# A float32 decoder trunk on one core: other start addresses for the matmuls' moving tiles, and gate and up products issued as three of 256 columns

## The chip, the cores and the metric

The kernel is one program on one core of a Trainium2 chip. The metric is the device time of one execution in microseconds (us), lower is better. In what follows PE is TensorE with its weight loads as PEld, DVE is VectorE, ACT is ScalarE, POOL is GpSimd, and SP is the engine that issues the weight transfers.

## The reference

Four layers work on 256 tokens of width 1024, all in float32. Each layer is a half-weighted SwiGLU feed-forward block, a token mixer, and a second feed-forward block:

```python
for i in range(DEPTH):                      # DEPTH = 4
    kind, j = i % N_MIXERS, i // N_MIXERS   # mixers: 0 gated DeltaNet, 1 stick-breaking, 2 sparse (DSA)
    x = x + 0.5 * swiglu(rmsnorm(x, ffn1_norm[i]), ffn1_w_gu[i], ffn1_w_down[i])
    h = rmsnorm(x, mix_norm[i])
    m = (gated_deltanet, stick_breaking_attention, dsa_sparse_attention)[kind](h, ...)
    x = x + m
    x = x + 0.5 * swiglu(rmsnorm(x, ffn2_norm[i]), ffn2_w_gu[i], ffn2_w_down[i])
return rmsnorm(x, final_norm)

def swiglu(h, w_gu, w_down):                # D_MODEL = 1024, D_FF = 2816
    gate, up = jnp.split(h @ w_gu, 2, axis=-1)
    return (jax.nn.silu(gate) * up) @ w_down
```

The mixers run in the order DeltaNet, stick-breaking, sparse, DeltaNet. Each has an input projection, attention-like work on 8 heads of 128, and an output projection 1024 to 1024.

## The kernel before

Everything is kept transposed, features on the 128 partitions and the 256 tokens along the free dimension. A float32 product is made exact enough from two float32r parts: an operand is split into `hi` and `lo`, and three products, `hi*hi + lo*hi + hi*lo`, are summed in PSUM. So each 128 by 128 weight tile with 256 tokens takes 768 columns of moving data.

**Weights.** Each chunk of 128 x 2048 weights (1 MB) arrives by one transfer on SP's queue into a tile `r` (3 buffers). It is split in four pieces of 512 columns: ACT writes `h` (L170), DVE writes `l` (L171), from pools `hi` and `lo` of 10 buffers each. A piece serves four k tiles of a gate or up product, or four row tiles of a down product.

**Activations.** `norm_in` writes x times the gain as one tile `x2` of 8 k tiles, each with 256 columns of hi beside 256 of lo; the trace calls it `x`. The hidden activations of a feed-forward block are `ah` and `al`, the heads' outputs of a mixer `oh` and `ol`, the latents of the sparse mixer `lath` and `latl`.

**Products.** The weight piece is the stationary operand and the activation the moving one. There are three forms:

- `tile_wide` makes the gate and up products: for each of 8 k tiles, the `h` weights against 512 columns (hi and lo of x side by side), then the `l` weights against 256 columns, into a PSUM bank of tag G.
- `rows` makes the down products and the output projections: for each tile three products of 256 columns (`mm3`), `ah` with `h`, `ah` with `l`, `al` with `h`. The same function serves the feed-forward blocks, which accumulate in four banks of tag A, and the mixers' `out_proj`, which accumulates `oh` and `ol` in four banks of tag G.
- `tiles2` makes the mixers' input projections: three products of 256 columns with `x2`, into banks of tag G.

Only the values of the stick-breaking mixer have it the other way round: there x is stationary and the weights move, 512 columns at a time.

**Order.** A feed-forward block is 11 steps of 256 hidden columns. A step (L346 to L361) is two chunks of gate and up products, 32 k tiles, and one chunk of down products of the step before, 48 products. Mixer work is written as generators that advance between groups of the big products (`pump`), by a count of PE's columns. Within an engine the instructions stand in the order that a scheduler gives them when the program is built; the engine then runs them in that order. The chain of small operations in a mixer is: rstd of the tokens, gates, keys with a triangular inverse, queries, the delta rule per head pair, then `out_proj`.

**Places in SBUF.** Tiles lie in pools, one behind the other. In the built program before, modulo 512 bytes, `h`, `l`, `x2`, `oh`, `ol`, `lath` and `latl` all start at 352, `ah` and `al` at 32, and the small weight tiles `bah`, `wih` and `wil` at 0. All slices that the big products take of them begin a multiple of 512 bytes further on, except in the sparse mixer's key projection.

Of the kernel before, what the change touches and what calls it, by code (L numbers as in the profile page):

```python
# [20 lines left out]
P = 128  # L21
T = 256          # tokens
D = 1024
KT = D // P      # k tiles of the model width
F = 2816
NS = F // 256    # steps of a feed-forward block, 256 hidden columns each
# [3 lines left out]
RS = 1024.0      # scale of the residuals kept in float16  # L30

# Everything is kept transposed: [feature on partitions, token].  A float32 matmul operand x is split
# exactly into hi = x rounded to float32r and lo = x - hi; hi*hi + lo*hi + hi*lo in PSUM carries float32.


class Bank:
    """One PSUM bank that several accumulation groups share."""
# [16 lines left out]
    def tr(self, out, x):  # L54
        """Transposes a [128, 128] float32 tile; the only kind of write to its part of the bank."""
        self.nc.tensor.transpose(out, x, self.k.ident)  # L56
        self.k.now += 0.11
# [8 lines left out]
class Trunk:  # L66

    def __init__(self, tc, ctx, a):
# [6 lines left out]
        self.lop = pool(name="lo", bufs=10)  # L75
        self.big = pool(name="big", bufs=8)
        self.wk = pool(name="wk", bufs=2)
# [20 lines left out]
    def table(self, name):  # L98
        """A mixer's constants, side by side."""
        t = self.wk.tile([P, 1024], F32, name="tab", tag="tab", bufs=1)  # L100
        src = self.a[name]
        self.nc.sync.dma_start(t[:, :src.shape[1]], src)
        return t
# [13 lines left out]
    def bank(self, tag="A"):  # L117
        """A: small products and a feed-forward's sums; G: the big projections."""
        return Bank(self, self.ps.tile([P, 512], F32, name="bank" + tag, tag=tag))

    # ---- interleaving: side work (generators) advances between groups of the big products.  A generator
    # yields how long (us on TensorE's clock, as counted here) its next stage's operands are expected to take,
    # or a condition that its next stage waits for.
# [6 lines left out]
    def pump(self, n=None):  # L130
        """Run up to n ready stages; only the first few (width) generators are under way."""
# [13 lines left out]
    def wait(self, done):  # L145
        """Run side work until done()."""
# [13 lines left out]
    def chunk(self, src, w=2048, pw=512, pool=(), parts=1):  # L160
        """A [128, w] chunk of weights as (hi, lo) pieces of pw columns; the pieces in pool are split by GpSimd."""
# [12 lines left out]
    def first_chunk(self, src, n):  # L174
        """The kernel's start: the first chunk and x arrive in parts and are split as they come."""
# [27 lines left out]
    def rsqrt(self, a, n):  # L203
        """Newton's iteration for a ** -0.5 on a small tile."""
# [20 lines left out]
    def norm_in(self, n):  # L225
        """x times the gain, split; the tokens' factors come later (rstd)."""
# [5 lines left out]
    def spread(self, cols):  # L232
        """[token, 1] columns (SBUF) -> a bank with each as a row on all partitions."""
# [5 lines left out]
    def rstd(self, st):  # L239
        """1 / rms(x) per token, into st: compact [token, 2] and as rows [128, T]."""  # L240
# [28 lines left out]
    # GDN's chunks of the input projection, (kind, head pair): keys 0, values 1, queries 2, gate 3  # L269
    gdn_order = ((0, 0), (0, 1), (0, 2), (3, 0), (0, 3), (3, 1), (2, 0), (1, 0), (1, 1), (1, 2), (1, 3),  # L270
                 (2, 1), (3, 2), (2, 2), (2, 3), (3, 3))
    korder = (0, 2, 4, 6, 1, 3, 5, 7)    # the order in which a block's last products finish x

    def tiles2(self, pieces, xg, order=None):
        """Two M tiles (8 k tiles each) of one chunk into one bank."""
# [8 lines left out]
    def tile_wide(self, pieces, m, order=None):  # L284
        """One M tile into a bank: the columns of hi * hi and those of hi * lo + lo * hi side by side."""
        b = self.bank("G")
        for q, j in enumerate(order or self.korder):
            wh, wl = self.sub(pieces, m * D + j * P, P)
            b.mm(b.t, wh, self.x2[:, j], False)
            b.mm(b.t[:, T:], wl, self.x2[:, j, :T], q == KT - 1)  # L290
# [4 lines left out]
    def rows(self, acc, pieces, a2, last, done=None):  # L295
        """acc[d, t] += w[f, d] a[f, t] for the chunk's two k tiles."""
# [910 lines left out]
```

## Time and profile before

| | |
|---|---|
| time, median of 3 runs | 2089.17 us (2088.93 to 2093.96) |
| the profiled execution: span from its first to its last instruction | 2092.3 us |
| PE busy | 97% of the span, 14762 matmuls |
| PEld, DVE, ACT busy | 90%, 79%, 63% |
| transfers | 353.62 MB, 169 GB/s on average |
| mean granted TensorE clock | 0.993 of full speed |

The span is the profiled execution's own time as far as it is listed. A busy share says how long an engine had something under way; matmuls overlap each other in it, so that what one matmul costs is read from the distance between the starts of two that follow each other, and not from its duration.

### The profile page before, as it was taken

What the parts mean: (1) busy time and instruction counts of PE and PEld (TensorE: products, weight loads), DVE (VectorE), ACT (ScalarE), POOL (GpSimd) and SP (SyncE); (2) the same over time, 40 slices, a digit from 0 to 9 for tenths busy, and PEclk for the clock granted to TensorE, in tenths of its full rate; (3) what the DMA queues carried; (4) which work ended last, traced back from release to release, by engine and by line L of the source; (5) the groups of instructions that cost most, each with busy time, mean ns of one, the idle gap of its engine ahead of it and who ended that gap; (6) DMA issues with size and microseconds to landing.
All of it is one profiled execution on the core that took longest, in us unless ns stands there. A gap on an engine that the chain in (4) does not pass through costs nothing.

```text
span 2092.3 us, 38898 instructions
## 1 busy us (share of the span) xinstructions
PE 2037.1 (97%) x14762; PEld 1886.2 (90%) x14762; DVE 1646.0 (79%) x3456; ACT 1308.2 (63%) x2804; POOL 161.9 (8%) x145
## 2 busy tenths in 40 slices
PE   8999899999999999999999998999999998999998
PEld 7999899999999989999989997899989998999997
DVE  7778898877887776777787789877787788988776
ACT  6566776665665566655665664765665667766654
POOL 1001311100100010100010013100010013111000
PEclk9999999999999999999999999999999999999999
DMA  7555333555455554555555542455555553235552
GB/s 256 195 188 182 102 105 123 173 190 187 171 206 188 195 179 140 176 184 197 185 184 199 182 153 76 162 187 196 184 182 199 184 179 106 100 119 182 182 199 84
DMA packets 52603, 353.62 MB, mean 169 GB/s; under 512 B 6976, under 2 KB 7872, under 8 KB 10688
## 3 DMA queue, kind: packets, MB, share of 16 engines
q1 hardware_dynamic: 52128, 350.49, 48.4%
q8 instruction: 116, 1.90, 0.4%
q14 instruction: 71, 0.58, 0.1%
q10 hardware_dynamic: 288, 0.66, 0.1%
HBM read 350.07 MB, written 1.05 MB: 168 GB/s over the span
## 4 chain that ended last, share of the span: by engine, by line
PE 82%; DVE 12%; ACT 4%; issue 1%; POOL 0%; DMA 0%; SPq 0%; ACTq 0%; DVEq 0%; POOLq 0%
PE bankG L43 55%; PE bankA L43 25%; DVE l L171 5%; ACT x L222 1%; DVE kT L466 1%; PE bankA L56 1%; ACT h L170 1%; DVE x L223 1%; DVE rs_t L211 1%; DVE x L302 0%; DVE rs_y L212 0%; DVE rs_t L210 0%; ACT sq L244 0%; DVE vT L466 0%; DVE pc L455 0%
## 5 line engine op out<-in xcount | busy, mean ns | idle before, releaser
L43 PE MATMUL bankG<-x,h 128*128 128x512 f32 (+1 forms) x4192 | 1269.0, 361 | 12.0 <-DVE x L223 12.0
L171 DVE TENSOR_TENSOR l<-r,h 128x512 fp32r<-128x512 f32 x1328 | 936.7, 713 | 374.1 <-ACT h L170 370.9
L170 ACT ACTIVATE h<-r 128x512 fp32r<-128x512 f32 x1328 | 823.0, 627 | 595.5 <-PE bankG L43 337.4
L43 PE MATMUL bankG<-x,l 128*128 128x256 f32 x3504 | 989.2, 282 | 0.0
L43 PEld LDWEIGHTS bankG<-x,h 128*128 128x128 f32 x4192 | 751.3, 189 | 130.1 <-DVE x L223 14.9
L43 PEld LDWEIGHTS bankG<-x,l 128*128 128x128 f32 x3504 | 666.5, 190 | 0.1
L43 PE MATMUL bankA<-ah,l 128*128 128x256 f32 x1408 | 389.2, 276 | 0.0
L43 PE MATMUL bankA<-ah,h 128*128 128x256 f32 x1408 | 389.2, 276 | 0.0
L43 PE MATMUL bankA<-al,h 128*128 128x256 f32 x1408 | 389.1, 276 | 0.0
L43 PEld LDWEIGHTS bankA<-ah,h 128*128 128x128 f32 x1408 | 264.4, 188 | 3.3
L43 PEld LDWEIGHTS bankA<-al,h 128*128 128x128 f32 x1408 | 264.5, 188 | 0.0
L43 PEld LDWEIGHTS bankA<-ah,l 128*128 128x128 f32 x1408 | 264.4, 188 | 0.0
L330 DVE TENSOR_TENSOR e<-e,bankG 128x256 f32<-128x256 f32 x352 | 145.9, 414 | 4.6 <-ACT e L329 4.6
L329 ACT ACTIVATE e<-bankG 128x256 f32<-128x256 f32 x352 | 129.3, 367 | 11.5 <-PE bankG L43 11.5
L245 POOL TENSOR_TENSOR sq<-sq 128x512 f32<-128x512 f32 x12 | 15.5, 1294 | 1473.8 <-ACT sq L244 1473.8
L342 DVE TENSOR_TENSOR e<-e,rb 128x512 f32<-128x512 f32 x176 | 121.0, 691 | 5.3 <-ACT rb L259 0.2
L199 ACT ACTIVATE ah<-e 128x256 fp32r<-128x256 f32 x176 | 72.6, 417 | 21.4 <-DVE e L344 21.3
L343 ACT ACTIVATE e<-e 128x256 f32<-128x256 f32 x176 | 71.3, 405 | 7.2 <-DVE e L342 7.2
L43 PE MATMUL bankG<-oh,h 128*128 128x256 f32 x256 | 74.5, 291 | 0.0
L344 DVE TENSOR_TENSOR e<-e 128x256 f32<-128x256 f32 x176 | 73.8, 419 | 0.7 <-ACT e L343 0.7
L200 DVE TENSOR_TENSOR al<-e,ah 128x256 fp32r<-128x256 f32 x176 | 73.1, 419 | 0.5 <-ACT ah L199 0.5
L43 PE MATMUL bankG<-oh,l 128*128 128x256 f32 x256 | 72.5, 283 | 0.0
(290 smaller groups left out, 1704.7 us busy)
## 6 DMA issues: line engine op xcount, KB each, us to landing
r<-in_ffn SPq DMA_DIRECT2D x262, 1024.0 KB, 4.9
r<-in_gdn_in SPq DMA_DIRECT2D x32, 1024.0 KB, 4.9
r<-in_gdn_out SPq DMA_DIRECT2D x8, 1024.0 KB, 4.9
r<-in_sb_qk SPq DMA_DIRECT2D x8, 1024.0 KB, 4.9
r<-in_sb_v SPq DMA_DIRECT2D x4, 1024.0 KB, 4.9
r<-in_sb_out SPq DMA_DIRECT2D x4, 1024.0 KB, 4.9
r<-in_dsa_out SPq DMA_DIRECT2D x4, 1024.0 KB, 4.9
r<-in_dsa_in SPq DMA_DIRECT2D x3, 1024.0 KB, 4.8
```

The costliest lines, as they stand in the source:

```text
L43: self.nc.tensor.matmul(out, lhsT, rhs, start=self.fresh, stop=stop, skip_group_check=True)
L56: self.nc.tensor.transpose(out, x, self.k.ident)
L170: self.nc.scalar.activation(h[:, :pw], src, AF.Copy)
L171: (self.nc.gpsimd if pool else self.nc.vector).tensor_sub(l[:, :pw], src, h[:, :pw].bitcast(F32))
L199: self.nc.scalar.activation(dh, src, AF.Copy)
L200: self.nc.vector.tensor_sub(dl, src, dh.bitcast(F32))
L211: nc.vector.scalar_tensor_tensor(t, t, -0.5, a, op0=ALU.mult, op1=ALU.mult)
L329: nc.scalar.activation(e[:, m * T:(m + 1) * T], b.t[:, :T], AF.Copy)
L330: nc.vector.tensor_add(e[:, m * T:(m + 1) * T], e[:, m * T:(m + 1) * T], b.t[:, T:])
L342: nc.vector.tensor_mul(e2, e2, st["rb"][:, None, :].to_broadcast([P, 2, T]))
L343: nc.scalar.activation(e[:, :T], e[:, :T], AF.Silu)
L344: nc.vector.tensor_mul(e[:, T:], e[:, T:], e[:, :T])
```

## The change

In `Trunk.__init__` the pool of working tiles (`wk`) now lies ahead of the pool of mixer tiles (`big`, which also holds `x2`), with a tile of 32 bytes between them. In the built program `x2`, `oh`, `ol`, `lath` and `latl` then start at 32 modulo 512 bytes. `h` and `l` stay at 352, `ah` and `al` at 32, and `bah`, `wih` and `wil` at 0; the large working tiles stay at 352.

`tile_wide` issues three products of 256 columns in place of one of 512 and one of 256. Some small tiles take the tag of another small tile, so that they share its buffers: `ks` that of `ms`, `qs` that of `gsp`, `dg`, `wx`, `fac` and `scl` those of `ea`, `beta`, `dl` and `ad`, `m8` that of `a4`; `mx` and `sm` become halves of one tile. Comments are gone, which moves line numbers by two to four.

```diff
@@ Trunk.__init__
+        self.wk = pool(name="wk", bufs=2)
+
+        pool(name="gap", bufs=1).tile([P, 8], F32, name="gap")
         self.big = pool(name="big", bufs=8)
-        self.wk = pool(name="wk", bufs=2)
@@ tile_wide
             wh, wl = self.sub(pieces, m * D + j * P, P)
-            b.mm(b.t, wh, self.x2[:, j], False)
-            b.mm(b.t[:, T:], wl, self.x2[:, j, :T], q == KT - 1)
+            xh, xl = self.x2[:, j, :T], self.x2[:, j, T:]
+            b.mm(b.t[:, :T], wh, xh, False)
+            b.mm(b.t[:, T:], wl, xh, False)
+            b.mm(b.t[:, T:], wh, xl, q == KT - 1)
...
-            ks = self.small("ks", [P, 2])
+            ks = self.small("ks", [P, 2], tag="ms")
...
-        qs = sm("qs")
+        qs = self.small("qs", [P, 4, 2, 2], bufs=1, tag="gsp")
...
-        dg = self.small("dg", [P, 6], bufs=1)
+        dg = self.small("dg", [P, 6], bufs=1, tag="ea")
...
-        wx = self.small("wx", [P, 16], bufs=1)
-        fac = self.small("fac", [P, 3, 2], bufs=1)
+        wx = self.small("wx", [P, 16], bufs=1, tag="beta")
+        fac = self.small("fac", [P, 3, 2], bufs=1, tag="dl")
...
-        scl = self.small("scl", [P, 2], bufs=1)
+        scl = self.small("scl", [P, 2], bufs=1, tag="ad")
...
-                parts.append((t, w, score[:, t, :w], self.small("m8", [P, 8])))
+                parts.append((t, w, score[:, t, :w], self.small("m8", [P, 8], tag="a4")))
...
-            mx, sm = self.small("mx", [P, 2], bufs=4), self.small("sm", [P, 2], bufs=4)
+            mx, sm = (lambda w: (w[:, :2], w[:, 2:]))(self.small("mx", [P, 4], bufs=4))
```

Three places show how the instructions stand. First PE, at the end of a step's gate and up products in the third step of the first feed-forward block, where the down products (`bankA`) begin. Before:

```order
L43 MATMUL bankG<-x_100,h 128x512
L43 MATMUL bankG<-x_100,l 128x256
L43 MATMUL bankA<-ah,h 128x256
L43 MATMUL bankA<-ah,l 128x256
L43 MATMUL bankA<-al,h 128x256
```

The same place of the change (`x_104` is `x2` again):

```order
L43 MATMUL bankG<-x_104,h 128x256 x2
L43 MATMUL bankG<-x_104,l 128x256
L43 MATMUL bankG<-x_104,h 128x256
L43 MATMUL bankA<-ah,h 128x256
L43 MATMUL bankA<-ah,l 128x256
L43 MATMUL bankA<-al,h 128x256
```

A k tile is now three products, the same form as the down products below it; the `x2` of the first row is the last product of one k tile and the first of the next. Apart from this, PE's order differs in two places at the start of the first block.

Second DVE, in a step of a feed-forward block: L171 splits weights, L330 adds the two halves of a gate or up product, L342 scales by the tokens' factor, L344 multiplies gate and up, L200 splits the result. Before:

```order
L171 TENSOR_TENSOR l<-r,h 128x512 x4
L330 TENSOR_TENSOR e<-e,bankG 128x256
L171 TENSOR_TENSOR l<-r,h 128x512 x2
L330 TENSOR_TENSOR e<-e,bankG 128x256
L342 TENSOR_TENSOR e<-e,rb 128x512
L171 TENSOR_TENSOR l<-r,h 128x512
L344 TENSOR_TENSOR e<-e 128x256
```

The same step of the change:

```order
L173 TENSOR_TENSOR l<-r,h 128x512 x3
L334 TENSOR_TENSOR e<-e,bankG 128x256
L173 TENSOR_TENSOR l<-r,h 128x512 x2
L334 TENSOR_TENSOR e<-e,bankG 128x256
L173 TENSOR_TENSOR l<-r,h 128x512
L346 TENSOR_TENSOR e<-e,rb 128x512
L173 TENSOR_TENSOR l<-r,h 128x512
L348 TENSOR_TENSOR e<-e 128x256
```

One split of weights has gone from ahead of the two additions to behind them. ACT's splits (L170) move in the same way.

Third SP's queue, around the DeltaNet layers: `dg` is a constant of the sparse mixer, `ad` one of the second DeltaNet layer. Before:

```order
L379 DMA ad<-in_gdn_ad 128x16
L381 DMA gn<-in_gdn_norm 128x1
L764 DMA dg<-in_dsa_gains 128x6
L164 DMA r<-in_ffn 128x2048 x3
L766 DMA wi<-in_dsa_widx 128x64
L164 DMA r<-in_ffn 128x2048 x22
L164 DMA r<-in_gdn_in 128x2048 x7
L379 DMA ad<-in_gdn_ad 128x16
L164 DMA r<-in_gdn_in 128x2048 x9
```

The same stretch of the change:

```order
L383 DMA ad<-in_gdn_ad 128x16
L385 DMA gn<-in_gdn_norm 128x1
L166 DMA r<-in_ffn 128x2048 x3
L770 DMA wi<-in_dsa_widx 128x64
L166 DMA r<-in_ffn 128x2048 x22
L166 DMA r<-in_gdn_in 128x2048 x7
L768 DMA dg<-in_dsa_gains 128x6
L166 DMA r<-in_gdn_in 128x2048 x9
```

`dg` now stands where the second `ad` stood, in the first DeltaNet layer, and the second `ad` has gone to the first weights behind the sparse mixer, between the second and the third chunk of `in_ffn`.

## Rows read from the trace of the kernel before

**Rows 1.** The page's first part: busy time, share of the span and instructions of an engine.

```profile
PE 2037.1 (97%) x14762; PEld 1886.2 (90%) x14762; DVE 1646.0 (79%) x3456; ACT 1308.2 (63%) x2804; POOL 161.9 (8%) x145
```

**Rows 2.** Busy time by stretch: the first DeltaNet mixer, one feed-forward block, the stick-breaking mixer, the sparse mixer. Columns: stretch, its length, busy time of each engine with the number of merged instructions, granted clock, share of the DMA engines, GB/s.

```profile
192.20:377.60 185.40, 175.02 (x1668) 169.56 (x1667) 165.91 (x439) 127.00 (x324) 40.43 (x36) 0.98 0.34 117
377.60:562.00 184.40, 183.88 (x1242) 168.50 (x1241) 143.00 (x270) 114.07 (x234) 5.34 (x4) 1.00 0.55 188
746.50:858.10 111.60, 109.42 (x786) 103.52 (x785) 71.38 (x141) 71.69 (x133) 5.30 (x4) 0.98 0.46 160
1227.00:1339.10 112.10, 101.00 (x722) 91.17 (x722) 95.31 (x269) 65.95 (x148) 29.10 (x25) 0.98 0.32 110
```

**Rows 3.** The chain that ended last, in order of time: the start of the kernel, and one step of the first feed-forward block. Columns: start, length, what.

```profile
11.29 14.11 PE bankG L43 x64
...
57.97 11.10 PE bankG L43 x64
69.07 5.45 PE bankA L43 x48
```

**Rows 4.** The timeline of PE over that step's 48 down products and the products on both sides. Columns here and in the timelines below: start, length, engine, line, operation, out<-in, shapes, count.

```profile
68.22 0.39 PE L43 MATMUL bankG<-x,h 128*128 128x512 f32 x1
...
68.56 0.39 PE L43 MATMUL bankG<-x,h 128*128 128x512 f32 x1
...
68.91 0.28 PE L43 MATMUL bankA<-ah,h 128*128 128x256 f32 x1
...
74.24 0.28 PE L43 MATMUL bankA<-al,h 128*128 128x256 f32 x1
```

**Rows 5.** The timeline of PE in the first DeltaNet mixer: input projection, then output projection. Between the first two rows lie 33 products.

```profile
200.08 0.40 PE L43 MATMUL bankG<-x,h 128*128 128x256 f32 x2
...
204.04 0.40 PE L43 MATMUL bankG<-x,h 128*128 128x256 f32 x2
...
362.96 0.28 PE L43 MATMUL bankG<-oh,h 128*128 128x256 f32 x1
...
363.92 0.28 PE L43 MATMUL bankG<-ol,h 128*128 128x256 f32 x1
```

**Rows 6.** The timeline of PE in the sparse mixer's index weights (nine products between the two rows) and in the stick-breaking mixer's values (three products of 512 moving columns of weights from row to row).

```profile
1244.84 0.39 PE L43 MATMUL bankA<-x,wih 128*8 128x256 f32 x2
...
1245.86 0.40 PE L43 MATMUL bankA<-x,wih 128*8 128x256 f32 x2
...
770.73 0.62 PE L43 MATMUL bankG<-h,x 128*128 128x512 f32 x2
...
771.41 0.62 PE L43 MATMUL bankG<-h,x 128*128 128x512 f32 x2
```

**Rows 7.** PE's groups of instructions, shapes kept apart: line, engine, operation, out<-in, shapes, count, busy time, mean ns of one, idle time before.

```profile
L43 PE MATMUL bankG<-x,h 128*128 128x512 f32 x2816 | 990.2, 394 | 11.7 <-DVE x L223 11.7
L43 PE MATMUL bankG<-x,l 128*128 128x256 f32 x3504 | 989.2, 282 | 0.0
L43 PE MATMUL bankG<-x,h 128*128 128x256 f32 x1376 | 278.9, 292 | 0.2 <-DVE x L223 0.2
L43 PE MATMUL bankG<-oh,h 128*128 128x256 f32 x256 | 74.5, 291 | 0.0
L43 PE MATMUL bankG<-lath,h 128*128 128x256 f32 x36 | 10.7, 297 | 0.0
```

**Rows 8.** The step of rows 3, busy time of each engine; who waited for whom in it (engine, tile, line, then us in total, times, longest); and DVE's group of the additions, columns as in rows 7.

```profile
57.97:74.52 16.55, 16.55 (x114) 15.23 (x113) 12.18 (x22) 9.91 (x21) 0.00 (x0) 1.00 0.57 193
...
DVE l L171 <- ACT h L170: 4.3, 6, 1.3
...
ACT h L170 <- PE bankG L43: 3.1, 3, 1.3
...
L330 DVE TENSOR_TENSOR e<-e,bankG 128x256 f32<-128x256 f32 x352 | 145.9, 414 | 4.6 <-ACT e L329 4.6
```

**Rows 9.** Busy time in stretches of the first DeltaNet mixer, and in the middle of the sparse mixer; columns as in rows 2.

```profile
232.00:302.00 70.00, 65.69 (x753) 62.49 (x752) 66.19 (x186) 50.37 (x122) 16.02 (x15) 1.00 0.24 79
...
1270.00:1310.00 40.00, 31.97 (x186) 25.68 (x185) 39.01 (x125) 20.08 (x48) 12.84 (x8) 0.96 0.18 61
```

**Rows 10.** The same stretches, the instructions on bank G alone (no POOL column); the second column's count is the big products in the stretch.

```profile
192.00:232.00 40.00, 26.27 (x197) 25.27 (x198) 2.05 (x3) 0.00 (x0) 0.96 0.35 122
232.00:302.00 70.00, 50.74 (x321) 41.68 (x320) 4.77 (x7) 0.00 (x0) 1.00 0.24 79
302.00:342.00 40.00, 31.76 (x235) 28.84 (x233) 3.42 (x5) 0.00 (x0) 1.00 0.52 186
342.00:352.00 10.00, 2.15 (x16) 1.80 (x14) 0.00 (x0) 0.00 (x0) 0.83 0.10 18
352.00:377.60 25.60, 21.55 (x167) 20.49 (x168) 1.11 (x3) 0.00 (x0) 1.00 0.42 147
1310.00:1339.00 29.00, 21.86 (x159) 20.13 (x160) 0.31 (x1) 0.26 (x1) 1.00 0.49 167
```

**Rows 11.** PE's waits in the first DeltaNet mixer, and in two feed-forward blocks: us in total, times, longest.

```profile
PE bankA L56 <- ACT kT L467: 3.1, 1, 3.1
PE bankA L56 <- ACT qT L467: 2.1, 1, 2.1
...
PE bankG L43 <- DVE x L223: 1.0, 2, 0.5
```

## The prediction

> **What bounds the kernel now.** I read the busy shares first. PE has 97%, its weight loads 90%, DVE 79% [rows 1]. By stretches this splits in two: in a feed-forward block PE is busy for 183.88 of 184.40 us and DVE for 143.00, so PE alone sets the end; in the DeltaNet mixer PE has 175.02 of 185.40 and DVE 165.91, and in the sparse mixer PE leaves 11 of 112 us idle [rows 2]. Eight blocks of 184 us are 70% of the span, and there the question is only how far apart two products start.
>
> That distance is the thing to see. In the chain, 32 k tiles of gate and up products take 11.10 us, 346.9 ns each for 768 columns, and 48 down products 5.45 us [rows 3]. In the timeline the 48 products with `ah` and `al` go from 68.91 to 74.24: 47 distances, 113.4 ns each [rows 4]; 5.45/48 gives 113.5, which I use. The mixers' products have the same 256 columns and the same weight tiles, but start 120 ns apart: 3.96 us for 33 with `x`, 0.96 us for 8 with `oh` [rows 5]. The output projection is made by the same function as the down products, in the same order. What is left between them is the PSUM tag (G against A) and where the moving tile starts: `ah` at 32 modulo 512 against weights at 352, `oh` and `x2` at 352 against weights at 352.
>
> Two more places help to choose. With `x2` at 352 against the small weight tile `wih` at 0, in a bank of tag A, nine products take 1.02 us, 113.3 each; so a moving tile at 352 isn't slow by itself. With weights moving, 512 columns at 352 against a stationary `x` at 352, three products into bank G take 0.68 us: 226.7 each, or 113.3 per 256 columns, so bank G isn't slow by itself either [rows 6]. The reading that fits is that a product of 256 columns loses 6.5 ns when its two operands start at the same place modulo 512. Why they disturb each other no row shows.
>
> **The change part by part.** *Gate and up products.* After the change `xh` and `xl` start at 32 against weights at 352, which is the down products' case in every respect but the bank: three products, three weight loads, `h`, `l`, `h`. I take 3 x 113.5 = 340.5 ns for a k tile in place of 346.9, 6.4 less. There are 2816 k tiles [rows 7], 32 in each of 88 steps: 2816 x 6.4 ns = 18.0 us. The very first step takes 14.11 us against 11.10 [rows 3], held by the clock and by arriving data, and I take its 0.2 us off: **17.8 us**. Bounds: 113.5 and 120 per product [rows 4, 5] give 340.5 and 360, from 18.0 us saved to 36.9 us lost. I take the first, since there the very same pair of addresses gives it.
>
> The Trainium skill speaks against this edit: "TensorE: Matmul & The Clock Gate", section "Back-to-back issue gap", gives an isolated gap of N/2.4 + 2.5 ns. By it a k tile would go from 325.0 to 327.5 ns, an estimate of 7.0 us lost over 2816. The trace doesn't agree: 113.5 ns and 346.9 ns both lie above its 109.2 and 325.0 [rows 3, 4].
>
> *Products of the mixers.* With `x2`: 1376 + 688, the latter being 3504 less the 2816 of `tile_wide`. With `oh` and `ol`: 3 x 256. With the latents: 3 x 36 [rows 7]; the key projection, whose weight slices begin elsewhere, is left out. Together 2940 x 6.5 ns = 19.1 us on PE, if all of it reaches the end. Bounds: nothing, and 19.1. It won't all arrive, since PE isn't alone there:
>
> - DeltaNet, twice. From 232 to 302 us DVE is busy for 66.19 of 70 [rows 9]: what PE gains on 321 products [rows 10] it waits for. The 197 products ahead of that run into the wait of 3.1 us for `kT`, behind the gates [rows 11]; that chain hangs on ACT, so their gain becomes wait as well. Behind it 235 + 16 + 167 = 418 products keep theirs: 2.7 us. The wait of 2.1 us for `qT` [rows 11] ends with a chain that PE's own product starts, so it comes earlier by as much. Twice 2.7 is 5.4 us.
> - Stick-breaking: PE is busy for 109.42 of 111.60, DVE for 71 [rows 2]. 384 + 192 products (8 chunks of two tiles, 8 k tiles and three products; the output projection) give 3.7 us.
> - Sparse: up to 1310 us DVE sets the pace, 39.01 of 40 [rows 9], and PE is idle for 8 of the 40. I count the 159 products after it [rows 10]: 1.0 us.
>
> That makes **10.1 us** of the 19.1.
>
> *The orders on DVE and ACT* change with the schedule: a split of weights now stands behind two additions. I cost it at nothing, because in a step ACT waits for PE to free a buffer before it can split (3.1 us in three waits) and DVE waits for ACT (4.3 us) [rows 8]; the splits are ahead by all of the ten buffers. A piece feeds 4 k tiles, 1.39 us, so ten are some 13.9 us of cover, against an addition of 0.41 us [rows 8] by which a split comes later. If that cover were gone, a step would pay up to 0.4 us for it, twice what it gains.
>
> *The start of a block.* The first product of a k tile no longer needs `xl` from DVE, but the third does. PE's wait for it is 1.0 us in two blocks [rows 11]; between 0 and 0.5 us per block could go. I take nothing.
>
> *Shared small tiles* cost no operation. They bring waits on SP: `dg` now waits for the first gates, `ad` for the sparse mixer's last exponentials, and weight transfers stand behind both. The raw buffers and the split pieces stand in between, and PE waits for the gates anyway (3.1 us for `kT`) [rows 11]. Bounds: nothing, and one such wait at each place, about 3 us together. I take nothing.
>
> *The clock.* After the wait for `qT` the granted clock of ten microseconds is 0.83 [rows 10], a third of them at 1.2 in place of 2.4 GHz, about 1.7 us of PE's work. That wait and its like stay as long or grow, so none of this comes back; a further wait that grew to two microseconds would cost as much again.
>
> **Sum.** 17.8 + 10.1 = 27.9 us from the profiled 2092.3 gives 2064.4. That execution is 3.1 us above the median of the three runs; the same amount from 2089.2 gives **2061 us**.
>
> **The rivals.** *The start address plays no part; bank G does.* Every 120 is in bank G [rows 5], both 113 with 256 columns are in A [rows 4, 6]. Then the mixers gain nothing and a k tile takes 3 x 120 = 360 ns: 13.1 x 2816 = 36.9 us lost, 2126 us. It decides from the point at which the three products take over 346.9 ns, 115.6 each. For it: no product of 256 columns in G is seen at 113.5. Against it: 226.7 for 512 columns in G [rows 6], and 0.34 us from 68.22 to 68.56 for a pair in G, which is less than 360 [rows 4].
>
> The Trainium skill supports this rival in "TensorE: Matmul & The Clock Gate", section "Step-by-step: what each phase is for": loading weights doesn't take read bandwidth from the running matmul, since there are two independent read ports, so where the tiles lie should not matter. No row here shows the ports; 113.5 against 120 from the same function speaks against it, if the bank isn't the reason.
>
> *The products gain as forecast, but other engines take half of it.* If a wait of 0.1 to 0.2 us enters each of 88 steps by the new order on DVE and ACT, 9 to 18 us go, and the time is 2070 to 2079. Against it stands DVE at 12.18 of 16.55 us in a step [rows 8].
>
> *The change doesn't do what it says for the wide products:* the three end at about 115.6 each, where the split saves nothing, and only the mixers' 10.1 us come: 2079.
>
> **How the numbers follow.** The likeliest, 0.77: 2061, with its own range from 2052 (all 18.0 + 19.1 arrive) to 2068 (the mixers keep a third, and the new waits on SP cost 3). Other engines take half: 0.10. No part of the address: 0.08, at 2126. Wide products unchanged: 0.05. Between them 0.05 fall within 0.3% (6.3 us) of before, taken from the second case at its worst; 0.3% is about what a measurement of this kernel can tell from no change. So faster 0.87, same 0.05, slower 0.08. The range for 8 in 10 reaches over the second and the last case and leaves out 2126: 2050 to 2080.
>
> **What would show it.** In the profile of the changed kernel a stretch of 32 k tiles in the chain should read 10.9 us and a step 16.35 in place of 16.55; `oh` and `x` products should start 113 to 114 ns apart; PE's waits in the DeltaNet mixers should grow by 2 to 3 us each while DVE's busy time stays. The prediction is wrong if `bankG` products of 256 columns still start 120 ns apart, or if PE shows waits inside a feed-forward block.

## The result, and the profile after

The changed kernel takes 2081.15 us (median of 12 executions, 2071.74 to 2089.53) where the kernel before takes 2090.43 (12 executions, 2087.84 to 2093.96) in the same comparison: the ratio is 0.9947, 95% interval 0.9933 to 0.9961. That is faster by 9.3 us, a third of the forecast 28, and outside the range of 2050 to 2080. The spread has grown too: 18 us between the lowest and the highest time, where before it is 6.

The profiled execution (2071.74 us) has a span of 2069.9 us. Its busy shares, from the page, answer to [rows 1]; then five stretches as in [rows 2], which are the first DeltaNet mixer, the feed-forward block behind it, the next feed-forward block, the stick-breaking and the sparse mixer.

```profile
PE 2006.7 (97%) x17578; PEld 1975.3 (95%) x17578; DVE 1611.2 (78%) x3456; ACT 1306.9 (63%) x2804; POOL 160.6 (8%) x145
```

```profile
189.20:372.40 183.20, 169.90 (x1669) 164.00 (x1669) 165.19 (x439) 126.90 (x324) 40.62 (x36) 0.99 0.33 118
372.40:560.70 188.30, 187.12 (x1592) 186.76 (x1592) 138.77 (x271) 114.07 (x233) 5.35 (x4) 1.00 0.52 185
560.70:742.90 182.20, 181.27 (x1595) 180.87 (x1594) 138.66 (x270) 113.89 (x233) 5.35 (x4) 1.00 0.54 192
742.90:850.10 107.20, 104.97 (x782) 99.19 (x781) 71.40 (x141) 71.44 (x133) 5.46 (x4) 1.00 0.46 163
1213.70:1325.60 111.90, 99.97 (x724) 89.92 (x723) 94.52 (x269) 65.78 (x149) 27.19 (x25) 0.98 0.32 111
```

The two feed-forward blocks hold the same work at the same full clock, and both leave PE idle for about 1 us (0.5 before, [rows 2]). Yet one takes 188.30 us and the other 182.20; before, both took some 184.4. The chain says why. These are steps of the first block (40.51), of the slow one (400.59, 406.24) and of the one behind it (588.50, 593.94), as in [rows 3]: start, length, what.

```profile
40.51 10.88 PE bankG L43 x96
51.38 5.44 PE bankA L43 x48
...
400.59 5.65 PE bankA L43 x48
406.24 11.31 PE bankG L43 x96
417.55 5.65 PE bankA L43 x48
...
588.50 5.44 PE bankA L43 x48
593.94 10.88 PE bankG L43 x96
```

96 products take 10.88 us, 113.3 ns each, or 11.31 us, 117.8 ns each, and the 48 down products behind them 5.44 or 5.65: 113.3 or 117.7. I call products that follow each other without a stop a string, and the time from the start of one to the start of the next its distance. So this string has two distances, a short one and a slow one, and a block keeps the one it got. The first two steps of a block hold stops; that leaves nine undisturbed stretches of gate and up products in each of the eight blocks. In this execution 63 of these 72 stand at 10.88 and 9 at 11.31, and all nine are this one block, a slow block from here on. Against [rows 3] a step of 16.55 us became 16.32 or 16.96.

Stage by stage, in us gained over the profiled execution of before: seven feed-forward blocks 2.1, 2.3, 2.6, 2.7, 2.3, 2.5 and 2.4; the eighth, at 372.4, lost 3.9; the DeltaNet mixers gained 2.2 and 1.6, stick-breaking 4.4, sparse 0.3. That makes 21.5; the other 0.9 of 22.4 lies ahead of the first stage mark.

PE's waits in the first DeltaNet mixer answer to [rows 11], and the timeline of its output projection to the rows of `oh` in [rows 5]:

```profile
PE bankA L56 <- ACT kT L471: 3.1, 1, 3.1
PE bankA L56 <- DVE rs_t L213: 2.7, 1, 2.7
PE bankA L56 <- ACT qT L471: 2.2, 1, 2.2
```

Of these the wait for `rs_t` was short before:

```profile
PE bankA L56 <- DVE rs_t L211: 0.8, 1, 0.8
```

The rows of `oh`:

```profile
356.80 0.28 PE L43 MATMUL bankG<-oh,l 128*128 128x256 f32 x1
...
358.04 0.28 PE L43 MATMUL bankG<-oh,h 128*128 128x256 f32 x1
```

From 356.80 to 358.04 lie eleven distances, 113 ns each, in bank G, where [rows 5] has 120.

### The profile page after: what moved, and what is told of

It is laid out like the page before. It is cut to its first block, busy times and chain, and to the rows that moved or that the text cites. A ratio compares the mean times of both kernels' runs of the same rounds, so it can differ in the third digit from the quotient of the medians.

```text
span 2069.9 us, 43693 instructions
## 1 busy us (share of the span) xinstructions
PE 2006.7 (97%) x17578; PEld 1975.3 (95%) x17578; DVE 1611.2 (78%) x3456; ACT 1306.9 (63%) x2804; POOL 160.6 (8%) x145
## 4 chain that ended last, share of the span: by engine, by line
PE 79%; DVE 15%; ACT 4%; issue 2%; POOL 0%; DMA 0%; SPq 0%; ACTq 0%; DVEq 0%; POOLq 0%
PE bankG L43 52%; PE bankA L43 26%; DVE l L173 6%; ACT x L224 1%; PE bankA L56 1%; DVE kT L470 1%; ACT h L172 1%; DVE x L225 1%; DVE rs_t L213 1%; DVE rs_y L214 1%; DVE x L306 1%; DVE rs_t L212 1%; DVE qT L470 0%; DVE e L334 0%; DVE vT L470 0%
## 5 line engine op out<-in xcount | busy, mean ns | idle before, releaser
L43 PE MATMUL bankG<-x,h 128*128 128x256 f32 x7008 | 1256.5, 280 | 10.0 <-ACT x L224 6.8
L43 PEld LDWEIGHTS bankG<-x,h 128*128 128x128 f32 x7008 | 1079.4, 189 | 12.4 <-ACT x L224 7.1
L43 PE MATMUL bankG<-x,l 128*128 128x256 f32 x3504 | 977.5, 279 | 0.0
L333 ACT ACTIVATE e<-bankG 128x256 f32<-128x256 f32 x352 | 133.7, 380 | 9.1 <-PE bankG L43 8.5
```

The costliest lines, as they stand in the source:

```text
L43: self.nc.tensor.matmul(out, lhsT, rhs, start=self.fresh, stop=stop, skip_group_check=True)
L333: nc.scalar.activation(e[:, m * T:(m + 1) * T], b.t[:, :T], AF.Copy)
```

## Experiments: which part does it

Eighteen runs were made; e1, m1 and p2 repeat a kernel. Behind each label stand times beside executions of the kernel before on the same chip. "Stretches" are the undisturbed ones of 32 k tiles (gate and up) and of 48 down products, 72 of each.

**The changed kernel again (e1_same).** No edit.

> The changed kernel once more, with a profile of another execution. Theory (a kept rate): a string of equal products, 256 columns each, keeps whichever of two rates it has when PE restarts after the wait at the transposes of rstd (113.3 or 117.8 ns a product) until PE waits again in the next block; so which of the eight feed-forward blocks run at 117.8 changes from execution to execution. Expected: other blocks than the second one are slow in this profile, each slow block about 188 us in place of 182, and times spread over 2065 to 2092 us in steps of about 7. Rival (bound to a place): the slow rate belongs to what happens in the second block (buffers, other engines' traffic); then the same block is slow here and no other, and the span is again 2070.

2072.71 us, ratio 0.9924 (0.9896 to 0.9952); its six times run from 2066.25 to 2086.32. Again 9 of 72 stretches at 11.31, again the block behind the first DeltaNet mixer. That is what the rival, a slow distance bound to this block, had forecast for the profile; the times, which spread over 20 us, speak against it, and the profiles of n2 and 288 below, with other slow blocks, end it. This block is still the commonest: it is slow in four of eight profiled executions of a kernel at this place or at 288 (the change, e1, 288, p2). One slow block costs ten steps of 0.43 + 0.21, 6.4 us. The lowest time, 2066.25, would then be an execution without one, and the median of all 18 times of this kernel, 2079.7, one with two; the executions without a profile don't show their blocks.

**The new places alone (e2_wide_kept).** `tile_wide` as before, the rest as changed:

```diff
-            b.mm(b.t[:, :T], wh, xh, False)
-            b.mm(b.t[:, T:], wl, xh, False)
-            b.mm(b.t[:, T:], wh, xl, q == KT - 1)
+            b.mm(b.t, wh, self.x2[:, j], False)
+            b.mm(b.t[:, T:], wl, self.x2[:, j, :T], q == KT - 1)
```

> The new places of the tiles alone: the gate and up products stay one of 512 columns and one of 256, all else is as in the changed kernel. Theory (a kept rate): the wide product changes the form of the string in every step, so no block stays at the slow rate beyond a step, and the times spread no more than before (about 6 us). The mixers keep what they gained in the profile of the changed kernel (2.2, 1.6, 4.4 and 0.3 us). If the pair still takes 346.9 ns the time is 2090.4 - 8.5 = 2082 us; if the new address makes the pair cheaper too, at most by 13 ns (120 against 113.3 for its second product, and as much for the wide one), the time goes down to 2082 - 37 = 2045. Rival (bound to a place): the second block's slow rate is here as well.

2115.95 us, ratio 1.0121 (1.0108 to 1.0134). Expected were 2082 or 2045; it is 25 us slower than before. Its steps read as these two rows of its chain, 71 of 72 down stretches at 5.65:

```profile
56.26 11.31 PE bankG L43 x64
67.56 5.65 PE bankA L43 x48
```

With wide products at 32 the slow distance is there always, also in the down products, whose own edit is nil. Before, with wide products at 352, the same down products took 5.45 [rows 3].

**Three products alone (e3_three_old_places).** The kernel before with the three products of the change, x2 at 352.

> Three products of 256 columns for gate and up, all tiles at the old places (moving and weight tiles both at 352 modulo 512 bytes). Theory (the address): each product starts 120 ns after the one before, a k tile takes 360 ns in place of 346.9, a stretch of 32 k tiles 11.5 us in place of 11.1, and the time is 2090 + 37 = 2127 us. Rival (the address matters only for bank G of the mixers): 113.4 ns a product as in the down products, 2090 - 18 = 2072 us.

2122.23 us, ratio 1.0155 (1.014 to 1.0169): 11.50 us for 96 products in all 72 stretches, 119.8 each, as the theory of the address had it (2127). Each half of the change by itself loses 25 to 32 us; only together do they gain.

**One wide product in eight (e4_one_wide_in_eight).** The changed kernel with the first k tile of each M tile wide.

```diff
+            if q == 0:
+                b.mm(b.t, wh, self.x2[:, j], False)
+                b.mm(b.t[:, T:], wl, xh, False)
+                continue
```

> The changed kernel, but the first of the eight k tiles of each gate and up tile is again one product of 512 columns and one of 256. Theory (a kept rate): the string is broken every 2.7 us, so that a slow rate lasts a part of a block at most; 352 wide k tiles cost at most 6.6 ns each, 2.3 us, and the time is near 2065 + 2.3 = 2067 us with a spread of a few us. Rival (bound to a place or to the execution, whatever the form): times as those of the changed kernel, 2072 to 2090.

2116.37 us, ratio 1.0123 (1.011 to 1.0136). I expected 2067. One wide product among 23 is enough: 71 of 72 down stretches at 5.65, every time within 2.4 us. Two rows of its chain:

```profile
57.05 11.31 PE bankG L43 x92
68.36 5.65 PE bankA L43 x48
```

The down products are untouched by this edit and slow down with the rest, so it isn't that each product has its own price: the string has a distance, and something sets it.

**The small tiles (n2_own_small_tiles).** The changed kernel with each small tile in buffers of its own again, and a gap of 64 bytes that keeps x2 and oh at 32:

```diff
-            ks = self.small("ks", [P, 2], tag="ms")
+            ks = self.small("ks", [P, 2])
...
-        dg = self.small("dg", [P, 6], bufs=1, tag="ea")
+        dg = self.small("dg", [P, 6], bufs=1)
```

> The changed kernel with the small tiles on buffers of their own again (ks, qs, dg, wx, fac, scl, m8, mx, sm as in the kernel before) and a gap of 64 bytes in place of 32, so that x2 and oh stay at 32 modulo 512. Theory of the prediction, sharing costs nothing: 2066 to 2080 us as the changed kernel, dg and ad loaded where they were. Rival, the shared buffers make SP or DVE wait in the mixers: the DeltaNet and sparse mixers become 1 to 3 us shorter each.

2081.34 us, ratio 0.9945 (0.9925 to 0.9965), the ratio of the change itself, 0.9947. The mixers gain 1.5, 2.9, 0.7 and -0.1 over before, no more than with shared tiles. Sharing costs nothing that these times, with an interval of 4 us to either side, can tell.

## Experiments: the place

The gap decides where the pool behind it starts: x2, oh, ol, lath, latl and the other tiles of that pool move together, and nothing ahead of it moves.

```diff
-        pool(name="gap", bufs=1).tile([P, 8], F32, name="gap")
+        pool(name="gap", bufs=1).tile([P, 24], F32, name="gap")
```

> The changed kernel with a wider gap: x2, oh and ol start at 96 modulo 512 (256 below the weights at 352 modulo 512 as a ring of 512); nothing else moves. Theory A, the difference of the two start addresses decides which distances there are: one of the four places 96, 160, 416, 480 gives another pair of distances than 113.3 and 117.8 ns; at this place either 113.3 in every block (all stretches of 32 k tiles 10.88 us, time 2066) or 117.8 and more. Theory B, only equal places modulo 512 matter: all four places behave as the changed kernel does, most blocks at 10.88, up to two of eight at 11.31, time 2066 to 2080.

> x2, oh and ol at 160 modulo 512, 192 below the weights at 352. Theory A: stretches of 32 k tiles other than in the changed kernel (all 10.88, or 11.31 and more in all). Theory B: as in the changed kernel, most blocks at 10.88, up to two at 11.31, 2066 to 2080 us.

> x2, oh and ol at 416 modulo 512, 64 above the weights at 352. Theory A: this place is nearest to the weights' and the likeliest to lose, 11.5 us for 32 k tiles as with equal places, time about 2120. Theory B: as in the changed kernel, 2066 to 2080 us.

> x2, oh and ol at 480 modulo 512, 128 above the weights at 352. Theory A: stretches of 32 k tiles other than in the changed kernel. Theory B: as in the changed kernel, most blocks at 10.88, up to two at 11.31, 2066 to 2080 us.

> x2, oh and ol at 288 modulo 512, 448 above (64 below) the weights at 352. From the five places so far (0 and 256 apart: 120 ns; 64 and 320: 117.8; 128: 119; 192: 113.3 with some blocks at 117.8) I expect a place that is 64 from the weights' to behave as 416 does: 11.3 us for 32 k tiles, about 2110. If the nearness matters by sign, 10.88.

> x2, oh and ol at 224 modulo 512, 128 below the weights at 352. If it is the mirror of 480 (128 above): 11.4 us for 32 k tiles, about 2117. If the order of the places matters by sign: 10.88 us, 2066 to 2080.

> x2, oh and ol at 64 modulo 512: 224 above the weights modulo 256. Between 192 (113.3 or 117.8 by blocks, at the places 32 and 288) and 0 (120). If the relation is one of 64 bytes and more, as at 192; if it is finer, another pair of distances, between 113.3 and 120.

> x2, oh and ol at 0 modulo 512: 160 above the weights modulo 256, between 128 (11.4 us for 32 k tiles) and 192 (10.88 or 11.31). Expected between: 11.3 in all, or as at 192.

Ten places are known with e3 and the change, ordered here by how far x2 starts behind the weights at 352, modulo 256:

| behind the weights, modulo 256 | x2 at (modulo 512) | 96 gate and up products, us | time, us |
|---|---|---|---|
| 0 | 352 (e3), 96 | 11.50, 11.50 | 2122, 2124 |
| 64 | 416, 160 | 11.31, 11.31 | 2111, 2112 |
| 128 | 480, 224 | 11.39, 11.39 | 2117, 2116 |
| 160 | 0 | 11.26 (54 of 72), 11.39 | 2111 |
| 192 | 32 (the change), 288 | 10.88 or 11.31 by blocks, both | 2081, 2086 |
| 224 | 64 | 11.35 | 2113 |

The four pairs of places that are 256 apart agree to the hundredth of a microsecond, so what counts here is the place modulo 256, not 512. I tell it as the difference from the weights; they stand at 352 in all ten, so that the moving tile's own place would fit these rows as well. Neither of my theories survives as it was put: "only equal places lose" falls, since seven of the nine other places lose as well, 18 to 32 us (ratios 1.009 to 1.015, every interval above 1); "the difference decides" holds, but modulo 256, and its guess that 416 would take 11.5 missed. The expectation that 288 would behave as 416 missed too. The place of the change is the only one that wins. The one 256 further on, 288, has the same two distances (45 stretches at 10.88, 27 at 11.31 in the profiled execution; 2086.39 us, ratio 0.9985, 0.9967 to 1.0002, the same as before), so no place tried has the short distance alone. A step of the chain at 96, where the down products behind have the short distance in all stretches but one:

```profile
58.73 11.50 PE bankG L43 x96
70.24 5.46 PE bankA L43 x48
```

And one at 160, in a block in which the slow distance stays:

```profile
412.59 11.31 PE bankG L43 x96
423.90 5.65 PE bankA L43 x48
```

At 96 and in e3 71 of 72 down stretches read 5.46, as they mostly do before: behind products at equal places, modulo 256, the string goes on at the short distance. That is the second half of the explanation. Behind the other slow places both distances follow: 5.45 in 26 of 72 down stretches at 160, 43 at 416, 54 at 480.

## Experiments: what sets a block

In the changed kernel PE stops in each block behind the first one at the two transposes that spread the tokens' factor (L56, `ident,rs_y`). The timeline of PE there, in the block at 372.4:

```profile
389.10 0.28 PE L43 MATMUL bankG<-x,l 128*128 128x256 f32 x1
389.21 0.28 PE L43 MATMUL bankG<-x,h 128*128 128x256 f32 x1
390.29 0.40 PE L56 MATMUL bankA<-ident,rs_y 128*128 128x128 f32 x2 [0.80 <-DVE rs_y L214]
390.45 0.36 PE L43 MATMUL bankG<-x,h 128*128 128x256 f32 x1
390.65 0.28 PE L43 MATMUL bankG<-x,l 128*128 128x256 f32 x1
...
391.00 0.28 PE L43 MATMUL bankG<-x,l 128*128 128x256 f32 x1
...
391.35 0.28 PE L43 MATMUL bankG<-x,l 128*128 128x256 f32 x1
```

Behind the stop a product with `l` follows the one before it after 0.35 us (three distances: 390.65, 391.00, 391.35), and so on to the end of the block; ahead of it that is 0.34 to 0.35, in detail 113.3 ns a product. In four profiled executions (the change, e1, n2, 288) eight blocks are slow: in five the string ran at 113 ahead of this stop, in three it was slow already. The stop works the other way too: five more blocks came to it at 117.8 and left it at 113.3 (in the change the block at 1325.6, behind a stop of 0.46 us).

**The stop taken away (n1_later_transposes, m1_later_again, p2_later_third).** The rstd chain is given more time, so that the transposes of seven blocks stand 18 products later (131 behind the block's start in place of 113, by the traces) and find their operand ready:

```diff
-    lat_sum, lat_newton = 5.2, 4.6
+    lat_sum, lat_newton = 5.2, 7.0
```

> The changed kernel with the delay of the rstd chain (lat_newton) at 7.0 in place of 4.6: PE issues the two transposes of a block's rstd some 12 products later, 1.4 us, so that their wait of about 1 us per block (0.7 to 0.8 in the rows of PE's waits) is gone and the string of products doesn't stop there. Theory 'the wait at the transposes is what the block's rate hangs on': no stop, no change of rate, all 72 stretches of 32 k tiles at 10.88 us, no steps of 6 to 7 us between executions; with 7 waits of 0.7 to 0.8 us gone, about 2061 us. Rival 'any break in the string can set it': blocks at 11.31 us remain, now one here, now one there, and only the waits are gained: 2066 to 2075 us.

> The same kernel as n1_later_transposes again. Theory 'a stop of PE at the transposes is the only thing that sets the slow distance': all 72 stretches at 10.88 us and 2059 to 2062 us, which the 2066, 2068 and 2081 of the first six times speak against. Rival 'any stop can set it, the one for x at a block's start too': times in steps of 6 to 7 us above 2060, the profile with whole blocks at 11.31 us in which the products ahead of the transposes already start 117.8 ns apart.

> n1_later_transposes a third time. Times again from 2060 to 2081 us in steps of 6 to 7 us. If the profiled execution has a block at 11.31 us, the products ahead of its transposes tell where it was set: 117.8 ns apart already there, then the start of x set it; 113.3 there, then the transposes did without a stop.

Three comparisons: 2063.41 us, ratio 0.988 (0.9853 to 0.9907); 2072.86, 0.9916 (0.9895 to 0.9937); 2067.03, 0.9882 (0.9867 to 0.9897). The 16 times run from 2060.11 to 2081.47, median 2067.2. In the first two profiled executions all 72 stretches are at 10.88. But the times keep their steps, so the theory that this stop alone sets a block fell. The third profiled execution caught a slow block; PE's timeline at its start, 12 us ahead of the transposes:

```profile
377.15 0.28 PE L43 MATMUL bankG<-x,l 128*128 128x256 f32 x1
...
377.49 0.28 PE L43 MATMUL bankG<-x,l 128*128 128x256 f32 x1
...
377.83 0.28 PE L43 MATMUL bankG<-x,l 128*128 128x256 f32 x1
378.48 0.50 PE L43 MATMUL bankG<-x,h 128*128 128x256 f32 x2 [0.37 <-DVE x L225]
378.81 0.28 PE L43 MATMUL bankG<-x,l 128*128 128x256 f32 x1
...
379.17 0.28 PE L43 MATMUL bankG<-x,l 128*128 128x256 f32 x1
...
379.52 0.28 PE L43 MATMUL bankG<-x,l 128*128 128x256 f32 x1
```

Here the stop is the one for `x`, and from product to product with `l` it is 0.34 us ahead (377.15, 377.49, 377.83) and 0.35 to 0.36 behind (378.81, 379.17, 379.52). The transposes of this block, without a stop, change nothing: 117.8 ahead of them and behind. So a stop of PE can set the distance, whichever stop it is; the same stop in n1's first profiled execution ended at 113.3.

**The waits by themselves (m2_before_later).** The same number in the kernel before.

> The kernel before with the delay of the rstd chain at 7.0. What is gained here is the waits alone: PE waits 0.27 us per block at the transposes there (distances of 378 and 300 ns against some 115), seven blocks, so 1 to 3 us: 2088 to 2090. If n1's gain over the changed kernel were due to the schedule and not to the blocks' distance, 5 us and more would go here too.

2086.86 us, ratio 0.9973 (0.9962 to 0.9984), 5.5 us less; I expected 1 to 3, and 5 and more if n1 gained by the schedule. By that measure the schedule has a part in n1's gain. Its feed-forward blocks are shorter by up to 0.9 us, the sparse mixer by 1.5 and the second DeltaNet mixer by 1.1. But the run doesn't show the waits by themselves: PE's recorded waits for `rs_y` are 12.0 us in 11 in both traces. What differs in a block is the string. Behind the stop, from 396 to 405 us, a k tile of before takes 353.5 ns on average and one of m2 346.8, and in m2 all 72 stretches are at 11.10 and all 72 down stretches at 5.45. So in the kernel before a stop could set a slower distance as well, for up to 27 us. The waits of the changed kernel can be read from its own traces. PE's waits for `rs_y` before, in the change and in n1:

```profile
PE bankA L56 <- DVE rs_y L212: 12.0, 11, 2.2
PE bankA L56 <- DVE rs_y L214: 18.3, 18, 2.2
PE bankA L56 <- DVE rs_y L214: 13.5, 11, 2.2
```

Seven waits, 4.8 us, are gone from the change to n1, and they make most of the 6.1 us between the lowest times of the two (2066.25 and 2060.11). The rest of n1's gain fits fewer slow blocks: its median lies 7.1 us above its lowest time, that of the change 13.4.

**Setting the string by hand (p1_four_equal).** n1 with four more products behind the transposes of each feed-forward block, with operands at equal places:

```diff
         s = self.spread([y[:, t:t + 1] for t in range(2)])
+        if same:
+            d = self.bank()
+            for j in range(same):
+                d.mm(d.t[:, :T], self.x2[:, j, :P], self.x2[:, j, :T], j == same - 1)
```

> n1_later_transposes with four more products behind the two transposes of rstd in each of the eight feed-forward blocks: 256 columns of x2 against 128 columns of x2 as weights, both at 32 modulo 512, into a bank that nothing reads (work added, the result of the kernel is untouched). Theory 'a string at equal places hands over at the short distance': no block at 11.31 us in any execution, all times within 3 us, at 2060 + 8 x 4 x 0.12 = 2064 us. Rival 'four products at 120 ns set nothing': times in steps of 6 to 7 us as before, from 2064 to 2085.

2067.46 us, ratio 0.9884 (0.9864 to 0.9903), four times from 2061.39 to 2070.06. One block of its profiled execution was slow ahead of the transposes. PE's timeline where the four products (`bankA<-x`) stand in it:

```profile
868.03 0.28 PE L43 MATMUL bankG<-x,l 128*128 128x256 f32 x1
...
868.39 0.28 PE L43 MATMUL bankG<-x,l 128*128 128x256 f32 x1
868.50 0.28 PE L43 MATMUL bankG<-x,h 128*128 128x256 f32 x1
868.62 0.38 PE L56 MATMUL bankA<-ident,rs_y 128*128 128x128 f32 x2
868.76 0.72 PE L43 MATMUL bankA<-x 128*128 128x256 f32 x4
869.32 0.28 PE L43 MATMUL bankG<-x,h 128*128 128x256 f32 x1
...
869.79 0.28 PE L43 MATMUL bankG<-x,l 128*128 128x256 f32 x1
...
870.13 0.28 PE L43 MATMUL bankG<-x,l 128*128 128x256 f32 x1
```

0.36 per three ahead (868.03, 868.39), 0.34 behind (869.79, 870.13), with no stop between: behind the four products the slow block went on at the short distance, and it stayed there. This is one block, and a stop ended the slow distance in five of eight cases; that equal places do it rests more on the down products of e3 and 96, 71 of 72 each. Four products at another place were not tried. Seven of eight blocks were fast. The eighth, the first one, was set behind them, by a stop between two down products: the rows of PE's timeline there stand at 34.65, 34.76, 34.88, and then at 35.05, after which the distance is 117.8. So the expectation that all times lie within 3 us missed, and in the profiled execution it is a later stop that undoes what the four products do. They bring nothing that can be seen: p1 (2067.46) and p2 (2067.03) stood on the same chip and don't differ.

## Why the prediction was wrong

*The direction was right, the mechanism in part.* The distance between two products hangs on where the moving tile starts, and bank G plays no part: `oh` at 113 and 96 products in 10.88 us, both in bank G. The rival of bank G (2126 us) falls with that. The rival in which other engines take half of the gain falls as it was put, since no wait enters the steps; but PE does show a wait of up to 0.8 us in a block, at the transposes, which the prediction had named as a sign of being wrong. The third rival, wide products that gain nothing, falls for a block at the short distance; in a slow block a k tile takes 353 ns and loses. The reading that a product is slow when both operands start at the same place modulo 512 was too narrow: seven of the nine other places lose as well. Place 32 was a good choice because its pair had been seen fast in the down products; that it differs from 352 would not have made it one.

*The sum was near for a block at the short distance, in part by luck.* A k tile takes 340 ns, forecast 340.5. Seven blocks gained 2.41 us on average, forecast 17.8/8 = 2.2. The mixers gained 8.5, forecast 10.1: DeltaNet 3.8 in place of 5.4, stick-breaking 4.4 in place of 3.7, sparse 0.3 in place of 1.0. PE's waits in the first DeltaNet mixer grew by 1.9 for `rs_t`, 0.3 for `rs_y` and 0.1 for `qT`, 2.3 together, forecast 2 to 3. Had the eighth block gained as much as the others, the stages would have given 27.8 us, forecast 27.9. These gains are read against the profiled execution of before, a long one; the lowest time, 2066.25, is only 24 us below the median of before. With the later transposes in both kernels, the profiled spans of m2 and of m1 (which has no slow block) lie 26.5 us apart, 2084.8 and 2058.3.

*The step that failed* is the price of a product: "I take the first, since there the very same pair of addresses gives it." That pair has a second distance, 117.8 ns, and I took the one row for the only one. The other was to be seen in the chain of before, where some down stretches take 5.65 or 5.66 (5 of 72), and one of them stands shortly before the stretch of [rows 3] that I read:

```profile
35.78 5.65 PE bankA L43 x48
41.43 11.10 PE bankG L43 x64
52.53 5.45 PE bankA L43 x48
...
589.88 5.66 PE bankA L43 x48
595.53 11.29 PE bankG L43 x64
606.83 5.45 PE bankA L43 x48
612.28 11.10 PE bankG L43 x64
```

In the kernel before the slow distance ends within two steps of the stop, in the gate and up products, whose operands start at equal places; at the places 96 and 352 the string goes on at the short distance behind such products. The change takes exactly these products away, and what a stop has set then lasts to the end of the block. That is worth 6.4 us a block. Of the 20 us between 2061 and 2081.15, 15 are put down to slow blocks (2081.15 less the lowest time, 2066.25), a little over two of 6.4; this is an estimate, since only the profiled executions show their blocks. What I called the risk, waits by the new order on DVE and ACT, was not where most of the gain went.

The other five lie in the last line of the sum. It took the span 2092.3 for a time 3.1 us above the median. Time and span lie 1.8 us apart in the execution shown above, so that execution of before is the slowest of its three, 2093.96, and 4.8 above the median. Less 27.9 that gives 2066.1, which is the lowest time to 0.2 us. So part of the agreement may come from that execution being long. The waits at the transposes, 4.8 us, which the sum has at nothing, are as large as this remainder; the two can't be told apart here.

*Costs taken at nothing.* Shared small tiles: n2 bears it out, to within 4 us. DVE's and ACT's new order: no wait of a split shows in a block. The start of a block was taken at nothing too; there the waits for the transposes grew (PE's waits for `rs_y` went from 12.0 us in 11 to 18.3 in 18), because the faster string reaches them earlier than the planner's delay assumes. In n1 they are 13.5 in 11.

The Trainium skill's "TensorE: Matmul & The Clock Gate", section "Step-by-step: what each phase is for", has the weight load on a read port of its own, so that it takes nothing from the running product. The runs show a dependence that this would not lead one to expect: by the start address of the moving tile alone, 96 products take from 10.88 to 11.50 us, at a granted clock of 1.00 in a block of either kind. Which access waits for which they don't show. The same page of the Trainium skill, section "Back-to-back issue gap", gives an isolated gap of N/2.4 + 2.5 ns, by which 256 columns take 109.2 ns, an estimate; the undisturbed strings of big products here show nothing below 113.3.

**What stays open.** Why the relation repeats after 256 bytes, and why 192 is the good one and 64, its mirror, is not, no run shows. Whether it is the difference of the two tiles or the moving tile's own place was not tried: the weights were never moved. Whether the slow distance comes from the exact moment at which PE starts again was not tried. What the four products need at least was not tried either.

## What to carry to other kernels

Where products follow each other without a gap, try several starts of the moving tile against that of the weights, since a gap tile costs only its bytes: the ten places here gave 2081 to 2124 us, and a place that merely differed was mostly no better. When a duration is read off one row, count all rows of its kind: a second value in a few of them is a state, and the question is what ends it in the old kernel, and whether the change takes that away. A faster string also reaches its waits earlier, so delays that a planner assumes have to move with it.

## What the runs showed of the hardware

- A string of products of 256 columns in float32r, each with a weight load of its own, has at a granted clock of 1.00 a mean distance of 113.3, 117.3 to 118.7 or 119.8 ns, by the place of the moving tile modulo 256 bytes (weights at 352 throughout). At 0, 64 and 480 single distances run from 115 to 123.
- At the difference of 192 there are two, 113.3 and 117.8 ns, and the string keeps the one it has through gate and up products and down products alike; up to 180 us of it were seen, to the block's end.
- A wide product (512 columns) of a tile at that difference sets the slow distance, one in 23 products is enough. Behind 96 products at equal places the 48 that follow are at the short distance, 71 of 72 times; behind four of them the one slow block that was seen went on at it.
- A stop of PE as short as 0.06 us (0.17 between the starts of two down products in place of 0.11) came with a change from 113.3 to 117.8, as stops of 0.4 and 0.8 us did; other stops of the same kind left the string at 113.3, and at the transposes five of eight slow strings came out at 113.3.
